# Two feed-forward blocks on one core: the down-projection of parts 2 and 3 as seven block products, added to x in DRAM

## The chip, the cores and the metric

One core of a Trainium2 chip runs the whole kernel. The metric is the device time of one execution in microseconds (us). The core has a matmul engine (PE), a vector engine (DVE), a scalar engine (ACT) and GpSimd (POOL), which all work on tiles in SBUF; PE writes its sums to PSUM banks. SP and POOL issue the transfers spoken of here.

## The reference

One layer of a language model for 512 prompt tokens and 8 sample tokens. A half-step feed-forward block stands before and after a mixer of attention and a state-space scan; only the two feed-forward blocks matter here.

```
def half_ffn(x, norm_g, w_in, w_out):
    h = rmsnorm(x, norm_g)
    gate, up = jnp.split(h @ w_in, 2, axis=-1)
    return x + FFN_RESIDUAL * ((jax.nn.silu(gate) * up) @ w_out)
...
        xp = half_ffn(xp, ffn1_norm[l], w_ffn1_in[l], w_ffn1_out[l])
...
        xp = xp + mixer_output(att, y_ssm, z, att_out_norm[l], ssm_out_norm[l], w_out[l])
...
        xp = half_ffn(xp, ffn2_norm[l], w_ffn2_in[l], w_ffn2_out[l])
```

FFN_RESIDUAL is 0.5, x has 1024 features, the hidden layer 2816, and everything is float32.

## The kernel before

x is kept transposed, as eight tiles of 128 features x 520 tokens, and the tokens are worked on in two halves of 260 (HF). A float32 product is made of three matmuls: both operands are cut into a high part (a cast by ACT) and a low part (what is left, a subtraction by DVE), and PE adds high x high, high x low and low x high in one PSUM bank. One matmul takes 128 x 128 weights and 260 columns.

A feed-forward block (`ffn_comb`) works through its 22 hidden blocks of 128 in four parts of 6, 6, 6 and 4 (PARTS). In each part the gate and up projections come first, block by block, then the down-projection of that part into all eight tiles of x. The first five hidden blocks (SFROM) are made by plain products. From the sixth on, the gate and up projections of a hidden block are one "pair": a 2 x 2 block product (two weight matrices, two token halves) of seven block products (`comb_pair`, `product`), as in the Strassen-Winograd scheme. Each of the seven has 4 x 3 = 12 matmuls; x, y and z are the PSUM banks that they add up in, tiles cx, cy and cz. ACT and DVE evict the banks between the products (L587 to L601). The fourth product of a pair is done one pair later (`comb_last`), and then ACT and DVE cut the finished hidden block into hidh and hidl (L612, L613).

The down-projection is plain: for each of eight outputs m, a loop over the hidden blocks k of the part and the two halves calls `mm3` (L222 to L224, tile fo), and DVE adds half of each bank to x (L468), which was loaded again into SBUF behind the first part (`reload`, tiles xr). That makes 8 x 6 x 2 x 3 = 288 matmuls for a part of six blocks. The last part of the first block runs with the mixer's opening (`to_mixer`, its weights in the tiles wraw, whi and wlo, L165, L191, L192); the last part of the second goes with the closing norm (`last_out`).

Weights come in units, a list made by `stream`: "cl" and "dn" plain ones, "pair" ones with seven weight combinations. A unit of a pair is loaded by SP as five raw tiles br; POOL adds up two of the sums by transfers that accumulate into SBUF (L348, L349), and DVE adds the other two (L381, L383; tile s). `b_split` cuts a unit into high parts qh (ACT, L354) and low parts ql (DVE, L355). Units are cut AHEAD = 10 us of matmul work before their use (`b_more`), and loaded at most two units ahead of the cuts. The raw tiles lie in a ring of 12, the cut ones in rings of 14 and 12 (pools pf and pg).

The order of PE's instructions is that of the program. The order on the other engines is set by a scheduler, within the dependencies, and each engine works through its row in order.

Of the kernel before, what the change touches and what calls it, by code (L numbers as in the profile page):

```python
# [14 lines left out]
T = 520  # L15
# [8 lines left out]
SRAW = 3  # L24
AHEAD = 10.0
# [57 lines left out]

def layout(inp):
# [5 lines left out]
    for n, s in (("ffn1", "1"), ("ffn2", "2")):  # L90
        out["wi" + s] = c(g[f"w_{n}_in"][0].reshape(8, 128, 2, 22, 128).transpose(3, 2, 1, 0, 4)).reshape(44, 128, 1024)
        out["wo" + s] = c(g[f"w_{n}_out"][0].reshape(22, 128, 8, 128).transpose(2, 1, 0, 3)).reshape(8, 128, 2816)
# [52 lines left out]
class Program:  # L145
# [147 lines left out]
    def stream(self, s):  # L293
# [3 lines left out]
        for lo, hi in PARTS:  # L297
            for j in range(lo, hi):
                if j < SFROM:
                    u += [("cl", wi[2 * j + i], 1024, 5.8) for i in range(2)]  # L300
                else:
                    u.append(("pair", wi[2 * j], wi[2 * j + 1], 10.1))
            if s == "1" and hi == PARTS[-1][1]:
                break
            u += [("dn", wo[m][:, lo * 128:hi * 128], (hi - lo) * 128, 0.72 * (hi - lo)) for m in range(8)]
# [6 lines left out]
    def q2(self, name):  # L312
# [6 lines left out]
        else:  # L319
            pool = self.pf if n < 12 or n % 7 % 2 == 0 else self.pg  # L320
        return pool.tile([128, 512], F32R, name=name, tag="q")

    def r2t(self, name):
        first = self.b_loaded <= 2 and self.b_first
        return (self.p0 if first else self.pf).tile([128, 512], F32, name=name, tag="r", bufs=4 if first else 12)

    def b_load(self):
# [15 lines left out]
        g, u = p  # L343
        h = slice(0, 512), slice(512, 1024)
        g0, s1, s3, g1, u1 = t = [self.r2t(f"br{n}_{i}") for i in range(5)]
# [12 lines left out]
    def b_split(self):  # L358
# [11 lines left out]
        else:  # L370
            g0, s1, s3, g1, u1 = raw
            s2, s4 = self.t2("s2"), self.t2("s4")
            w = {}
            ends = self.b_cut == len(self.bu), self.b_cut == len(self.bu) - 1
            if self.b_first == 0 and any(ends):
                self.qpool = self.pf
            w[1], w[5] = self.cut(g0), self.cut(s1)
            if self.b_first == 0 and ends[0]:
                self.qpool = self.pg
            w[2] = self.cut(g1)  # L380
            nc.vector.tensor_add(s2[:, :512], s1, g0)  # L381
            w[6] = self.cut(s2)
            nc.vector.tensor_add(s4[:, :512], s2[:, :512], g1)  # L383
            w[3], w[7] = self.cut(s4), self.cut(s3)
            if self.b_first == 0 and ends[1]:
                self.qpool = self.pg
            w[4] = self.cut(u1)
# [15 lines left out]
    def ffn_comb(self, gcol, source, after=None, early=None):  # L403
# [3 lines left out]
        with self.tc.manual_schedule(engines={mybir.EngineType.PE}):  # L407
            hid, held, r, norm = [], None, None, None
            for j in range(SFROM):
                pair = []  # L410
                if j == 0:
# [6 lines left out]
                    if self.b_first:  # L418
                        self.leave("p0")
                        self.enter("pg", 12, "right")  # L420
# [23 lines left out]
            prev = None  # L444
            for part, (lo, hi) in enumerate(PARTS):
                for j in range(max(lo, SFROM), hi):
                    prev = self.comb_pair(j, prev, hid)
                last = part == len(PARTS) - 1
# [1173 lines left out]
```

## Time and profile before

| | us |
|---|---|
| three runs | 1106.94, 1107.76 (median), 1111.99 |
| profiled execution, its own time | 1109.26 |
| its span in the profile | 1107.5 |
| PE busy | 1073.4 |
| DVE busy | 719.4 |
| ACT busy | 501.4 |
| POOL busy | 264.6 |

The first feed-forward block lies at about 5 to 374 us of the span, the mixer behind it to about 735, the second block from there to about 1092. A matmul's record lasts longer than the distance to the next one, so distances are read from starts. The time from issue to landing of a transfer counts until its end is known to the engine that waits for it.

### The profile page before, as it was taken

Reading aid. Unit: us, or ns where it says so; the run is one execution under the profiler, and the core shown is the slowest. Engines: PE = TensorE matmul, PEld = TensorE weight load, DVE = VectorE, ACT = ScalarE, POOL = GpSimd, SP = SyncE. Lnnn points to the kernel's source line nnn. Section 1 sums busy time; section 2 is a strip of 40 time slices with the busy share of each in tenths; the row PEclk is TensorE's granted clock in tenths of the full one; section 3 lists DMA queues with packets and bytes.
Section 4 is the critical chain, followed back from the end, with each engine's and each line's share of the span. In section 5 each row is a group of like instructions: output and inputs, shape, how many; then the busy total and the mean of one; then the engine's idle time right before and its main releaser. Section 6 shows DMA issues by size and latency. Waiting matters only on the chain.

```text
span 1107.5 us, 23255 instructions
## 1 busy us (share of the span) xinstructions
PE 1073.4 (97%) x9079; PEld 991.7 (90%) x9079; DVE 719.4 (65%) x1499; ACT 501.4 (45%) x1077; POOL 264.6 (24%) x261
## 2 busy tenths in 40 slices
PE   8999999999999999999999998999999999999995
PEld 6999999999999988776756676999999999999995
DVE  6985477467555679363768868449855764685563
ACT  6452355256244422456622555245534543562452
POOL 0001001110105667575343321120020011101013
PEclk9999999999999999999999999999999999999997
DMA  8539358455616788688899735163484584556302
GB/s 272 136 104 255 92 144 222 107 139 170 161 47 205 269 305 298 232 281 305 292 379 406 268 131 197 47 221 99 133 226 104 131 232 98 147 176 150 109 11 78
DMA packets 93917, 204.30 MB, mean 184 GB/s; under 512 B 13384, under 2 KB 21960, under 8 KB 89712
## 3 DMA queue, kind: packets, MB, share of 16 engines
q1 hardware_dynamic: 68736, 124.19, 34.4%
q0 software_dynamic: 22336, 77.08, 24.6%
q10 hardware_dynamic: 2736, 1.56, 0.5%
q8 instruction: 71, 1.16, 0.4%
q14 instruction: 38, 0.31, 0.1%
HBM read 191.78 MB, written 11.01 MB: 183 GB/s over the span
## 4 chain that ended last, share of the span: by engine, by line
PE 86%; DVE 5%; DMA 3%; issue 2%; ACT 2%; POOL 1%; ACTq 0%; DVEq 0%; SPq 0%; POOLq 0%
PE fo L223 7%; PE fo L224 7%; PE fo L222 7%; PE cx L578 6%; PE cx L577 6%; PE cx L576 6%; PE mps L222 4%; PE mps L223 3%; PE mps L224 3%; PE gu L222 3%; PE gu L224 3%; PE gu L223 3%; PE cy L576 3%; PE cy L577 3%; PE cy L578 3%; PE sps L1060 2%
## 5 line engine op out<-in xcount | busy, mean ns | idle before, releaser
L354 ACT CAST qh<-br 128x512 fp32r<-128x512 f32 (+1 forms) x310 | 168.2, 585 | 120.0 <-PE fo L223 57.5
L355 DVE TENSOR_TENSOR ql<-br,qh 128x512 fp32r<-128x512 f32 (+1 forms) x310 | 188.8, 644 | 44.1 <-ACT qh L354 19.3
L223 PE MATMUL fo<-hidl,qh 128*128 128x260 f32 x640 | 181.3, 283 | 0.8 <-DVE hidl L613 0.8
L222 PE MATMUL fo<-hidh,qh 128*128 128x260 f32 x640 | 181.1, 283 | 0.0
L224 PE MATMUL fo<-hidh,ql 128*128 128x260 f32 x640 | 180.8, 283 | 0.0
L578 PE MATMUL cx<-ch,ql 128*128 128x260 f32 x544 | 153.8, 283 | 0.0
L577 PE MATMUL cx<-cl,qh 128*128 128x260 f32 x544 | 153.6, 282 | 0.0
L576 PE MATMUL cx<-ch,qh 128*128 128x260 f32 x544 | 153.5, 282 | 0.0
L223 PEld LDWEIGHTS fo<-hidl,qh 128*128 128x128 f32 x640 | 120.4, 188 | 1.6 <-DVE hidl L613 1.5
L222 PEld LDWEIGHTS fo<-hidh,qh 128*128 128x128 f32 x640 | 120.5, 188 | 0.0
L224 PEld LDWEIGHTS fo<-hidh,ql 128*128 128x128 f32 x640 | 120.5, 188 | 0.0
L222 PE MATMUL mps<-hh,whi 128*128 128x260 f32 x384 | 113.3, 295 | 2.3 <-DVE raw L880 2.3
L348 POOL DMA_DIRECT2D br<-in_wi x34 | 29.7, 874 | 354.7 <-DMA br<-in_wi 204.7
L223 PE MATMUL mps<-hl,whi 128*128 128x260 f32 x384 | 109.7, 286 | 0.6 <-DVE hl L233 0.6
L224 PE MATMUL mps<-hh,wlo 128*128 128x260 f32 x384 | 109.4, 285 | 0.0
L576 PEld LDWEIGHTS cx<-ch,qh 128*128 128x128 f32 x544 | 102.4, 188 | 0.0
L578 PEld LDWEIGHTS cx<-ch,ql 128*128 128x128 f32 x544 | 102.4, 188 | 0.0
L577 PEld LDWEIGHTS cx<-cl,qh 128*128 128x128 f32 x544 | 102.3, 188 | 0.0
L786 POOL DMA_INDIRECT kv<-in_kc,ix x66 | 74.0, 1122 | 59.5 <-PE cy L578 25.7
L222 PEld LDWEIGHTS mps<-hh,whi 128*128 128x128 f32 x384 | 73.3, 191 | 13.5 <-issue 10.4
L577 PE MATMUL cy<-cl,qh 128*128 128x260 f32 x272 | 77.0, 283 | 0.0
L576 PE MATMUL cy<-ch,qh 128*128 128x260 f32 x272 | 76.9, 283 | 0.0
(430 smaller groups left out, 2705.4 us busy)
## 6 DMA issues: line engine op xcount, KB each, us to landing
br<-in_wi SPq DMA_DIRECT2D x206, 256.0 KB, 3.9
br<-in_wi POOLq DMA_DIRECT2D x68, 256.0 KB, 4.7
br<-in_wo SPq DMA_DIRECT2D x56, 256.0 KB, 2.9
wraw<-in_wm SPq DMA_DIRECT2D x24, 512.0 KB, 6.3
br<-in_wo SPq DMA_DIRECT2D x48, 128.0 KB, 2.7
kv<-in_kc SPq DMA_DIRECT2D x22, 256.0 KB, 4.6
spill<-xr SPq DMA_DIRECT2D x16, 260.0 KB, 3.3
xr<-spill SPq DMA_DIRECT2D x16, 260.0 KB, 5.5
```

The lines of the kernel that those rows point to most:

```text
L222: mm(out, lhsT=hi[:, ks], rhs=xh[:, cs], start=start, stop=False)
L223: mm(out, lhsT=hi[:, ks], rhs=xl[:, cs], start=False, stop=False)
L224: mm(out, lhsT=lo[:, ks], rhs=xh[:, cs], start=False, stop=stop)
L348: nc.gpsimd.dma_start(s1, u[:, h[1]], accum_op=ALU.add)
L354: self.nc.scalar.copy(hi[:, :n], raw[:, :n])
L355: self.nc.vector.tensor_sub(lo[:, :n], raw[:, :n], hi[:, :n])
L576: mm(out, lhsT=hi[:, ks], rhs=xh, start=start and i == 0, stop=False, skip_group_check=True)
L577: mm(out, lhsT=hi[:, ks], rhs=xl, start=False, stop=False, skip_group_check=True)
L578: mm(out, lhsT=lo[:, ks], rhs=xh, start=False, stop=i == 3, skip_group_check=True)
L786: nc.gpsimd.indirect_dma_start(out=pages[j], out_offset=None, in_=a["kc"], in_offset=bass.IndirectOffsetOnAxis(ap=self.ix[:, 4 * n + j:4 * ...
L1060: nc.tensor.matmul(self.sbank[32 * hp:32 * hp + 32, cs], lhsT=self.qz[:, c0:c0 + 32], rhs=rhs(hp), start=(n % 16 == 0), stop=(n % 16 == 15 ...
```

## The change

The down-projections of the second and third part (COMB, each six hidden blocks) of both feed-forward blocks are made of seven block products too (`down_comb`). Here the 2 x 2 blocks are two outputs m and m+1 by two hidden blocks, times two hidden blocks by two token halves. A part has three pairs of hidden blocks and four pairs of outputs; each of the seven products has 3 x 3 = 9 matmuls into the tiles dx, dy and dz. `hidden` makes the seven operand combinations from two finished hidden blocks, in place of hidh and hidl; the rows of the output weights are put into that order on the host (`hidden_order`). The work of `down_comb` stands behind the first pair of the next part, and the tail's fourth product is done within its first output pair.

The results x0 and x1 (tiles xs, a ring of four) are no longer added to x in SBUF. ACT and DVE evict them, scaled by 0.5 or -0.5, and POOL adds them to x in DRAM (`spill`) by accumulating transfers. The first part's down-projection loads each x tile for its addition and stores it to `spill`; x is reloaded from there before the last part. The products within a pair have a new order, 1, 5, (4 of the pair before), 2, 6, 3, 7, and `combos` copies one more operand (eight ACT copies). The rings shrink: raw tiles 12 to 10, cut tiles 14 to 11 and 12 to 9; xs (4) and the DVE sums (2) get rings of their own.

The core of the diff:

```
+COMB = (1, 2)
...
-            u += [("dn", wo[m][:, lo * 128:hi * 128], (hi - lo) * 128, 0.72 * (hi - lo)) for m in range(8)]
+            if part in COMB:
+                return [("pair", w[m], w[m + 1], n // 2, 1.26 * (hi - lo)) for m in range(0, 8, 2)]
+            return [("dn", w[m], n, 0.72 * (hi - lo)) for m in range(8)]
...
                 for j in range(max(lo, SFROM), hi):
-                    prev = self.comb_pair(j, prev, hid)
...
+                    prev = self.comb_pair(j, prev, hx if prev and j == lo else hid, comb)
+                    if j == lo and todo is not None:
+                        self.down_comb(hx, prev, hid)
...
+                if last:
+                    self.reload(self.spill)
...
+                    xm = self.x[m] if last else self.x_load(m, source)
...
                     if not last:
+                        nc.sync.dma_start(self.spill[m], xm[:, :T])
...
+    def down_comb(self, hx, tail, hid):
...
+        for m in range(0, 8, 2):
+            w = self.b_take()
+            x, y, z = (self.bank1(n)[:, :HF] for n in ("dx", "dy", "dz"))
+            x0, x1 = (self.px.tile([128, 528], F32, name=f"xs{m + i}", tag="x") for i in range(2))
+            pu = self.t2("pu")
+            self.product(x, w, 1, True, hx)
+            nc.scalar.copy(z, x)
+            self.product(y, w, 5, True, hx)
+            nc.scalar.activation(pu[:, a], y, AF.Copy, scale=-0.5)
+            if m == 0:
+                self.comb_last(tail, hid)
+            self.product(x, w, 6, False, hx)
+            nc.scalar.activation(pu[:, b], x, AF.Copy, scale=0.5)
+            self.product(z, w, 2, False, hx)
+            nc.scalar.activation(x0[:, a], z, AF.Copy, scale=0.5)
+            self.product(x, w, 7, False, hx)
+            stt(x1[:, b], x, -0.5, pu[:, a], ALU.mult, ALU.add)
+            self.product(y, w, 3, False, hx)
+            stt(x0[:, b], y, 0.5, pu[:, b], ALU.mult, ALU.add)
+            nc.gpsimd.dma_start(self.spill[m], x0[:, :T], accum_op=ALU.add)
+            self.product(x, w, 4, False, hx)
+            nc.scalar.activation(x1[:, a], x, AF.Copy, scale=-0.5)
+            nc.gpsimd.dma_start(self.spill[m + 1], x1[:, :T], accum_op=ALU.add)
+            self.b_more()
...
+    def hidden(self, c, hx):
...
+        x0, x1 = hx.pop()[0], c
+        p1 = self.t2("p1", F32R)
+        nc.scalar.copy(p1[:, a], x0[:, a])
+        nc.vector.tensor_sub(p1[:, b], x0[:, a], p1[:, a])
+        s, t = self.t2("hs"), self.t2("ht")
+        nc.vector.tensor_sub(s[:, a], x0[:, a], x0[:, b])
+        nc.vector.tensor_sub(s[:, b], x1[:, b], x0[:, b])
+        nc.vector.scalar_tensor_tensor(t[:, a], s[:, b], -1.0, x0[:, a], ALU.mult, ALU.subtract)
+        nc.vector.scalar_tensor_tensor(t[:, b], t[:, a], -1.0, x1[:, a], ALU.mult, ALU.subtract)
+        q = self.two(s, x1, t)
```

How it moves the rows, at three places. First ACT in the first block, down-projection of part 2. Before, the row there is casts of weights alone (br raw tiles, s sums of them):

```order
196 L354 CAST qh<-br_1_2701 128x512 [waits DMASW6_49,Activation_49]
197 L354 CAST qh<-br_3_2703 128x512 [waits DMAHW0_49,PE_49,Activation_49]
198 L354 CAST qh<-s_2812 128x512 [waits DVE_49,PE_49,Activation_49]
199 L354 CAST qh<-s_2813 128x512 [waits DVE_49,PE_49,Activation_49]
200 L354 CAST qh<-br_2_2702 128x512 [waits DMASW7_49,PE_49,Activation_49]
201 L354 CAST qh<-br_4_2704 128x512 [waits DMAHW2_49,PE_49]
202 L354 CAST qh<-br_1_2761 128x512 [waits DMASW0_49,PE_49,Activation_49]
```

Now, from the end of the pair ahead on, with the first evictions of the first output pair:

```order
211 L374 CAST qh<-br_1_2540 128x384 [waits DMASW2_49,PE_49]
212 L374 CAST qh<-br_3_2542 128x384 [waits DMAHW2_49,PE_49,Activation_49]
213 L374 CAST qh<-s_2714 128x384 [waits PE_49]
214 L526 COPY dz<-dx 128x260
215 L374 CAST qh<-s_2715 128x384 [waits DVE_49,PE_49]
216 L528 ACTIVATE pu<-dy 128x260
217 L374 CAST qh<-br_2_2541 128x384 [waits DMASW3_49,PE_49]
218 L532 ACTIVATE pu<-dx 128x260 [waits PE_49]
219 L534 ACTIVATE xs_2761<-dz 128x260 [waits PE_49]
```

The evictions of dx, dy and dz stand between the casts of the weights for the next units, and a cast that waits for PE is ahead of the copy into dz.

Second POOL at the same place. Before, it issues only the accumulating transfers for weight sums:

```order
22 L348 DMA br_1_2701<-in_wi 128x512 [waits DMAHW3_49,DMAHW7_49,DMASW3_49,DVE_49]
23 L349 DMA br_2_2702<-in_wi 128x512 [waits DMAHW1_49,DMAHW5_49,DMASW7_49,DVE_49]
24 L348 DMA br_1_2761<-in_wi 128x512 [waits DMAHW0_49,DMAHW4_49,DMASW5_49,DVE_49]
25 L349 DMA br_2_2762<-in_wi 128x512 [waits DMAHW2_49,DMAHW6_49,DMASW1_49,DVE_49]
26 L348 DMA br_1_2845<-in_wi 128x512 [waits DMAHW1_49,DMAHW5_49,DMASW2_49,DVE_49]
```

Now those and the additions to x in DRAM take turns:

```order
30 L368 DMA br_1_2747<-in_wo 128x384 [waits DMAHW3_49,DMASW2_49,DVE_49]
31 L539 DMA spill<-xs_2761 128x520 [waits DVE_49,Activation_49]
32 L369 DMA br_2_2748<-in_wo 128x384 [waits DMAHW5_49,DMASW3_49]
33 L542 DMA spill<-xs_2762 128x520 [waits Activation_49]
34 L368 DMA br_1_2882<-in_wi 128x512 [waits DMAHW0_49,DMASW4_49,DVE_49]
35 L539 DMA spill<-xs_2896 128x520 [waits DVE_49,Activation_49]
36 L369 DMA br_2_2883<-in_wi 128x512 [waits DMAHW2_49,DMASW5_49]
37 L542 DMA spill<-xs_2897 128x520 [waits Activation_49]
```

Each addition to x waits for evictions by ACT or DVE, and the next transfer for a weight sum stands behind it.

Third SP's queue at the end of the first block, where the weights of the last down-projection (wraw) are loaded. Before, they follow the raw tiles of the last pair:

```order
232 L347 DMA br_3_4348<-in_wi 128x512 [waits DMAHW5_49,DVE_49,Activation_49]
233 L347 DMA br_2_4347<-in_wi 128x512 [waits DMAHW6_49,DMASW4_49,Activation_49]
234 L347 DMA br_4_4349<-in_wi 128x512 [waits DMAHW7_49,DVE_49,Activation_49]
235 L165 DMA wraw_4734<-in_wo 128x512 [waits DMAHW0_49,DMASW6_49,DMAHW3_49,DVE_49,Activation_49]
236 L165 DMA wraw_4736<-in_wo 128x512 [waits DMAHW1_49]
```

Now the eight reloads of x stand ahead of them:

```order
249 L367 DMA br_2_4534<-in_wi 128x512 [waits DMAHW6_49,DMASW0_49,DVE_49]
250 L367 DMA br_4_4536<-in_wi 128x512 [waits DMAHW7_49,DVE_49]
251 L1551 DMA xr_4975<-spill 128x520 [waits DMAHW0_49,DMASW3_49,PE_49]
252 L1551 DMA xr_4976<-spill 128x520 [waits DMAHW1_49,DMASW5_49,PE_49]
253 L1551 DMA xr_4977<-spill 128x520 [waits DMAHW2_49,DMASW7_49,PE_49]
254 L1551 DMA xr_4978<-spill 128x520 [waits DMAHW3_49,DMASW1_49,PE_49]
255 L1551 DMA xr_4979<-spill 128x520 [waits DMAHW4_49,DMASW3_49,PE_49]
256 L1551 DMA xr_4980<-spill 128x520 [waits DMAHW5_49,DMASW5_49,PE_49]
257 L1551 DMA xr_4981<-spill 128x520 [waits DMAHW6_49,DMASW7_49,PE_49]
258 L1551 DMA xr_4982<-spill 128x520 [waits DMAHW7_49,DMASW1_49,PE_49]
259 L175 DMA wraw_4999<-in_wo 128x512 [waits DMAHW0_49,DMASW4_49,DVE_49]
```

The first load of wraw waits for DVE in both; its place in the memory of the cut tiles is another one now, because the rings are shorter, and the DVE instruction that frees it is the low part of the last pair's last cut.

## Rows read from the trace of the kernel before

**Rows 1.** Page: busy us of each engine, then the chain that ended last.

```profile
PE 1073.4 (97%) x9079; PEld 991.7 (90%) x9079; DVE 719.4 (65%) x1499; ACT 501.4 (45%) x1077; POOL 264.6 (24%) x261
...
PE 86%; DVE 5%; DMA 3%; issue 2%; ACT 2%; POOL 1%; ACTq 0%; DVEq 0%; SPq 0%; POOLq 0%
```

**Rows 2.** Page, costliest groups: busy us, mean ns, idle before; L222 and L224 alike.

```profile
L223 PE MATMUL fo<-hidl,qh 128*128 128x260 f32 x640 | 181.3, 283 | 0.8 <-DVE hidl L613 0.8
L222 PE MATMUL fo<-hidh,qh 128*128 128x260 f32 x640 | 181.1, 283 | 0.0
```

**Rows 3.** Timeline of PE, first matmuls of products: start us, duration us.

```profile
147.49 0.28 PE L576 MATMUL cy<-ch,qh 128*128 128x260 f32 x1
...
148.94 0.28 PE L576 MATMUL cz<-ch,qh 128*128 128x260 f32 x1
...
151.81 0.28 PE L576 MATMUL cx<-ch,qh 128*128 128x260 f32 x1
```

**Rows 4.** Windows, one pair and one down-projection: us, busy, clock, DMA share, GB/s.

```profile
134.50:144.60 10.10, 10.10 (x86) 10.10 (x85) 7.67 (x15) 6.13 (x13) 0.86 (x1) 1.00 0.58 158
...
182.09:215.90 33.81, 33.81 (x281) 33.81 (x282) 16.26 (x33) 7.60 (x14) 5.02 (x6) 1.00 0.59 131
```

**Rows 5.** Timeline of PE, start of part 2's down-projection, idle in brackets.

```profile
181.32 0.28 PE L222 MATMUL fo<-hidh,qh 128*128 128x260 f32 x1
182.09 0.39 PE L223 MATMUL fo<-hidl,qh 128*128 128x260 f32 x1 [0.49 <-DVE hidl L613]
```

**Rows 6.** Timeline of ACT in the same pair as rows 3.

```profile
147.47 0.61 ACT L354 CAST qh<-br 128x512 fp32r<-128x512 f32 x1
147.99 0.37 ACT L587 COPY cz<-cx 128x260 f32<-128x260 f32 x1
...
152.01 0.38 ACT L593 COPY pu<-cx 128x260 f32<-128x260 f32 x1 [0.98 <-PE cx L578]
```

**Rows 7.** Groups of 100 to 340 us by form: busy us, mean ns.

```profile
L354 ACT CAST qh<-br 128x512 fp32r<-128x512 f32 x93 | 54.2, 619 | 36.3 <-PE fo L223 17.9 <-issue 13.5 <-PE fo L224 3.0
L354 ACT CAST qh<-br 128x256 fp32r<-128x256 f32 x16 | 6.5, 403 | 4.7 <-DMA br<-in_wi 2.4 <-PE fo L223 2.2
...
L355 DVE TENSOR_TENSOR ql<-br,qh 128x512 fp32r<-128x512 f32 x95 | 62.0, 684 | 13.8 <-PE fo L224 4.9 <-ACT qh L354 3.8 <-issue 1.8
L468 DVE SCALAR_TENSOR_TENSOR xr<-fo,xr 128x260 f32<-128x260 f32 x44 | 17.0, 424 | 17.0 <-PE fo L224 17.0
L355 DVE TENSOR_TENSOR ql<-br,qh 128x256 fp32r<-128x256 f32 x16 | 6.7, 417 | 1.7 <-PE cx L577 1.4 <-issue 0.3
```

**Rows 8.** Line L165 at 330 to 360 us: the last part's weight loads.

```profile
L165 SPq DMA_DIRECT2D wraw<-in_wo x7: 327/338/423, 337.5 to 357.4; - x7
...
DMA to landing us min/median/max: 4.3/4.4/4.4
```

**Rows 9.** Timeline of PE, first matmul of the first block's last down-projection.

```profile
347.42 0.28 PE L222 MATMUL fo<-hidh,whi 128*128 128x260 f32 x1
```

**Rows 10.** Page, DMA queues and issues (KB each, us to landing).

```profile
q1 hardware_dynamic: 68736, 124.19, 34.4%
q0 software_dynamic: 22336, 77.08, 24.6%
...
br<-in_wi SPq DMA_DIRECT2D x206, 256.0 KB, 3.9
br<-in_wi POOLq DMA_DIRECT2D x68, 256.0 KB, 4.7
br<-in_wo SPq DMA_DIRECT2D x56, 256.0 KB, 2.9
...
spill<-xr SPq DMA_DIRECT2D x16, 260.0 KB, 3.3
xr<-spill SPq DMA_DIRECT2D x16, 260.0 KB, 5.5
```

**Rows 11.** Page, costliest groups: POOL issuing the weight sums, 874 ns each.

```profile
L348 POOL DMA_DIRECT2D br<-in_wi x34 | 29.7, 874 | 354.7 <-DMA br<-in_wi 204.7
```

More of the change, by code (lines that the diff above doesn't have):

```diff
@@ L81, in shape_constants, with hidden_order @@
     return f, b.astype(mybir.dt.np(BF16)), i3, r
+def hidden_order():
+    o = []
+    for part, (lo, hi) in enumerate(PARTS):
+        o += [j for i in range(2) for j in range(lo + i, hi, 2)] if part in COMB else range(lo, hi)
+    return o
 def layout(inp):
@@ L296, in stream, with down @@
         u = []
-        for lo, hi in PARTS:
+        def down(part):
+            lo, hi = PARTS[part]
+            n = 128 * (hi - lo)
+            w = [wo[m][:, lo * 128:hi * 128] for m in range(8)]
+            if part in COMB:
+                return [("pair", w[m], w[m + 1], n // 2, 1.26 * (hi - lo)) for m in range(0, 8, 2)]
+            return [("dn", w[m], n, 0.72 * (hi - lo)) for m in range(8)]
+        for part, (lo, hi) in enumerate(PARTS):
             for j in range(lo, hi):
@@ L301, in stream @@
                 else:
-                    u.append(("pair", wi[2 * j], wi[2 * j + 1], 10.1))
-            if s == "1" and hi == PARTS[-1][1]:
-                break
-            u += [("dn", wo[m][:, lo * 128:hi * 128], (hi - lo) * 128, 0.72 * (hi - lo)) for m in range(8)]
+                    u.append(("pair", wi[2 * j], wi[2 * j + 1], 512, 10.1))
+                if j == lo and part - 1 in COMB:
+                    u += down(part - 1)
+            if part not in COMB and not (s == "1" and hi == PARTS[-1][1]):
+                u += down(part)
         self.bu = u
@@ L324, in r2t @@
         first = self.b_loaded <= 2 and self.b_first
[L325 removed]
+        return (self.p0 if first else self.pf).tile([128, 512], F32, name=name, tag="r", bufs=4 if first else 10)
     def b_load(self):
@@ L567, in combos, with product @@
         halves(self.two(*tt), 6, 4)
-    def product(self, out, w, p, start):
+    def product(self, out, w, p, start, blocks):
         mm = self.nc.tensor.matmul
         hi, lo = w[p]
-        for i in range(4):
-            xh, xl = self.cx[i][p]
+        last = len(blocks) - 1
+        for i, block in enumerate(blocks):
+            xh, xl = block[p]
             ks = slice(128 * i, 128 * i + 128)
@@ L577, in product, with comb_pair @@
             mm(out, lhsT=hi[:, ks], rhs=xl, start=False, stop=False, skip_group_check=True)
-            mm(out, lhsT=lo[:, ks], rhs=xh, start=False, stop=i == 3, skip_group_check=True)
-    def comb_pair(self, j, prev, hid):
+            mm(out, lhsT=lo[:, ks], rhs=xh, start=False, stop=i == last, skip_group_check=True)
+    def comb_pair(self, j, prev, hid, comb):
         nc = self.nc
@@ L1575, in early @@
             def early():
+                self.leave("py")
                 self.leave("pg")
@@ L1601, in run @@
                 self.ffn_comb(V_F2, self.spill)
-            self.leave("pg")
-            self.leave("pf")
+            for n in ("py", "pg", "px", "pf"):
+                self.leave(n)
 def kernel(**inputs):
```

111 lines of the change are left out of this document (72 added, 39 removed).

## The prediction, made before the changed kernel had run

> **What bounds the kernel now.** I read the page's engine shares and its chain first [rows 1]: the matmul engine is busy 97% of the span and 86% of the chain that ended last lies on it. So in the two feed-forward stages time is the number of matmuls times their pitch, unless something makes PE wait. Then the costliest groups [rows 2]: the down-projection is three groups of 640 matmuls, with 0.8 us of waiting in all. The 283 ns printed there overlap, so they are not the price of one. The price is in the timeline of a block product [rows 3]: 12 matmuls from 147.49 to 148.94, and 12 more to each next start (151.81 is two products later), so 1.44 us / 12 = **0.120 us** each. Last I looked at what DVE and ACT do in a stretch of pairs and in a down-projection [rows 4], because the change buys matmuls with work on those two.
>
> **What it removes.** A down-projection of six hidden blocks is 8 outputs x 6 blocks x 2 halves x 3 = 288 matmuls; in seven products it is 4 output pairs x 7 products x 3 block pairs x 3 = 252. Parts 2 and 3 of both stages do it: 4 x 36 = 144 matmuls fewer, 144 x 0.120 = **-17.3 us**. All 144 stood in stretches where PE hardly waited, so all of it is on the path. At the old down-projection of part 2 PE also waited at 181.32 to 182.09 for the last hidden block's low part [rows 5], 0.77 instead of 0.12: **-0.65 us**, since the products now run one pair later, when the hidden blocks have long been ready.
>
> **What it adds to the path: evictions in less cover.** Within a pair, a product that starts from an evicted bank has one product of 12 matmuls as cover, 1.44 us. ACT's copy starts 0.20 us after the next product's first matmul (152.01 against 151.81) and lasts 0.38 [rows 3, 6]; when a cast is ahead of it, it starts later (147.99 against 147.49, behind the cast of 147.47) and ends at 148.36, 0.87 us after the product's end, 0.58 before it is needed at 148.94. In the new down-projection a product has 9 matmuls, 1.08 us. The order of ACT shows the tight spot: a cast of a weight sum, then the copy of dx into dz, which the sixth product, on the same bank, needs. By the analogue the margin is 1.08 - 0.87 = 0.21 us, less if the cast (384 columns, between 0.403 and 0.619 us [rows 7], estimate 0.51) is itself released late: it waits for a DVE sum or for a slot that the first product frees. It is tight in 12 of the 16 output pairs (in the other four the tail's product stands between). Bounds: 0 where the margin holds; a whole cast late, 0.51 x 16 = 8 us. The analogue row, which holds, is nearer: I take **+1.5 us**. The other evictions have a product or more of cover and no cast that must be ahead.
>
> **The step into the mixer.** Before, the first weight of the last down-projection was issued at 337.5 and landed 4.4 us later, though its first matmul came only at 347.42: 5 us of slack [rows 8, 9]. After, the order of SP's queue has that load behind the eight reloads of x and on a wait for DVE, and the wait resolves to the low part of the last unit's last cut, whose slot (of 9 instead of 12) is freed by the product into cz of the last pair. From that product's end to the first down matmul there are 3 products and a matmul, 37 x 0.120 = 4.5 us. What has to fit: the cut 0.69, issue about 0.1, landing 4.4, the cast 0.62 and the subtraction 0.69 [rows 7, 8], 6.5 us, and the low part is wanted two matmuls after the high one, at 4.7. So it is about 6.5 - 4.7 = **+1.8 us** late, once (the second stage takes its last weights another way); 0 if the landing is the 2.9 of other such loads [rows 10] and the cut is early, 3 at most if DVE is late by another instruction or two.
>
> **What lies under other work, at nothing.** (1) DVE. Two hidden blocks were two subtractions of 520 columns, about 0.69 each; now five of 260 (0.424 each, by the eviction's row) and three of 520: 4.2 against 1.4 us, +1.4 per pair. A pair had 7.67 of 10.10 us busy, so 9.1 of 10.1: 90%. In a down-projection an output pair costs seven subtractions and two sums of 384 columns (0.55 each, estimate between 0.417 and 0.684) and two evictions, 5.8 of its 63 x 0.120 = 7.56 us [rows 4, 7]. These records overlap at their ends, so both fit; what covers them is the look-ahead of about one pair (10 us) in the cut weights, and when it is gone each pair loses what DVE is over. (2) ACT: seven casts of 0.51 and five copies of 0.38 are 5.5 of 7.56 us. The eight copies added where the first stage's products are set up cost 8 x 0.38 = 3 us of ACT, beside a longer DVE chain. (3) Transfers. An output pair loads five tiles of 0.197 MB, accumulates into two of them, and sends two tiles of 0.266 MB to x. At what the queues did while busy (124.19 MB in 34.4% of 1107.5 us, 0.326 MB/us; 77.08 MB in 24.6%, 0.283 MB/us [rows 10]) that is 0.98/0.326 + 0.93/0.283 = 6.3 of 7.56 us: 83%, against 59% in the old down-projection [rows 4]. No row shows an accumulate whose destination is DRAM. From below, it costs no more than a plain store, 3.3 us to landing; from above, twice the time on the engines for reading and writing there: 1.9 us more per output pair, 8.2 of 7.56, a deficit of 2.5 us over the four, under the look-ahead. I take nothing, as stores to DRAM landed sooner (3.3) than loads from it (5.5) [rows 10]. The Trainium skill speaks against that ("DMA: Bandwidth & Descriptors", section "Anatomy of one DMA — SWDGE (gpsimd) path"): a transfer reports done only when its last byte is confirmed, and this "can cause a surprisingly long delay especially when the write target is HBM"; the trace's 3.3 against 5.5 us doesn't show it for stores. (4) POOL: 0.874 us per issue [rows 11], four per output pair, 3.5 of 7.56 us; a spill accumulate waits for its evictions and holds the next weight accumulate behind it for some 2 to 3 us, which the look-ahead also covers. (5) The shorter ring of raw tiles (10 for 12, two units): a load can start only a unit ahead, about 10 us, and needs 3.9 to 4.7 [rows 10] and the accumulates behind it as much again: 1 to 2 us to spare.
>
> **Sum.** -17.3 - 0.65 + 1.5 + 1.8 = -14.65 us. The profiled execution took 1109.26 us (span 1107.5 and 1.76 around it), so 1094.6; the median of the three runs is 1107.76, 1.5 less, which gives **1093 us**.
>
> **Rivals.**
> A, the forecast, with its bounds: losses of 0 to 11 us instead of 3.3. At nothing it is 1089.8; the runs of before spread from 1106.94 to 1111.99, so 1087 to 1099. Chance 0.62.
> B, PE stutters at the evictions: cover of 1.08 us is too little not at one product in seven but at two, 0.4 us each, 16 output pairs: +13 over the clean 1089.8, about 1103 (1099 to 1106). For it: 0.21 us is all the margin, and a cast ahead holds the copy, as at 147.99. Against: ACT is busy only 73% there. Chance 0.16.
> C, DVE or the transfers become the bound and the saved matmuls turn into waits: DVE at 90% in a pair, where it must also answer PE; if each of the 24 pairs in the four parts loses 0.7 us, 17 us are given back and nothing is won, about 1106 to 1109. This is also the case in which the change does what it says, and it doesn't matter. Against: DVE sat idle 2.4 us of each pair before. Chance 0.13.
> D, slower: the accumulates into DRAM land late. The ring for their sources has four tiles, two per output pair, so a tile is wanted again 2 x 7.56 = 15.1 us after its first write; some 3 us go to the other eviction and the issue, so up to 12 us to landing costs nothing. The nearest rows are 3.3 (store) and 4.7 (accumulate into SBUF) [rows 10], and both would have to be far off. From 12 us it decides: ACT's and DVE's evictions wait for the tile, their casts queue behind, PE runs dry. At 20 us the last two output pairs of each part wait 8 us, times 4 is 32, less if the look-ahead eats some: 1089.8 + 32 = about 1120. By the page of the Trainium skill named above, a destination in HBM would push towards this. Chance 0.09.
>
> **How the numbers follow.** The forecast is A's 1093. The range must leave out no more than two in ten: from 1087 to 1106 it takes A and B and leaves C's half and D above. Half a per cent, what a measurement of this kernel can tell from no change, is 1102.2 to 1113.3: A and a part of B fall below it, the rest of B and C inside, D above. Faster 0.76, same 0.15, slower 0.09.
>
> **What would show it.** Right: 144 matmuls fewer, pitch 0.120 in the groups of the new down-projection, an output pair of 7.6 us, a wait of 1 to 2 us before the first matmul of the last part in the first stage, small gaps at the sixth product released by ACT's copy into dz. Wrong: gaps at other products (B), PE waiting for the low parts of weights with DVE busy without a break (C), ACT or DVE idle on the spill accumulate and its landing far above 5 us (D). What would break the forecast most is a transfer to DRAM that adds at another speed than it stores.

## The result

The changed kernel is slower. Its runs have a median of 1115.51 us (1111.28 to 1124.27, 17 runs), the kernel before one of 1107.82 us in 17 runs; the ratio is 1.0069 with a 95% interval of 1.0049 to 1.0088, so 8 us lost where 15 were forecast to be won. The time lies outside the range that I gave. The profiled execution has a span of 1117.9 us; its own time, 1119.96 us, is 4.5 us above the median, so its waits are somewhat longer than those of a middle run.

The page of the changed kernel: busy us of each engine, the DMA queues (packets, MB, share of 16 engines), the chain that ended last, the transfers (KB each, us to landing). They answer to [rows 1] and [rows 10].

```profile
PE 1066.6 (95%) x8935; PEld 980.2 (88%) x8935; DVE 778.8 (70%) x1619; ACT 570.4 (51%) x1245; POOL 319.2 (29%) x325
...
q1 hardware_dynamic: 75648, 135.85, 37.3%
q0 software_dynamic: 31552, 91.90, 32.9%
...
PE 76%; DMA 9%; DVE 6%; issue 4%; POOL 3%; ACT 2%; DVEq 0%; SPq 0%; ACTq 0%; POOLq 0%
...
br<-in_wi SPq DMA_DIRECT2D x206, 256.0 KB, 4.4
br<-in_wi POOLq DMA_DIRECT2D x68, 256.0 KB, 5.3
...
spill<-xs POOLq DMA_DIRECT2D x32, 260.0 KB, 7.4
```

The 144 matmuls are gone (8935 against 9079), yet PE's share of the chain fell from 86% to 76%, and DMA's rose from 3% to 9%. So PE now waits. The list of waits says for whom (us in total, times, longest); first PE's two that were not there before, then DVE's behind them:

```profile
PE dx L654 <- DVE xs L536: 11.9, 6, 3.7
PE cx L654 <- DVE pu L678: 5.3, 4, 2.0
```

```profile
DVE s L402 <- DMA br<-in_wi: 40.6, 13, 5.9
```

The first line of PE's is in the new down-projections; the second is in the gate/up pairs, and comes back below. The largest wait of all, at the last output pair of the first block's part 2, shows the whole chain. PE, then DVE, then POOL, from the timeline (start us, duration us, idle before in brackets; rows left out between):

```profile
217.61 0.28 PE L656 MATMUL dy<-ch,ql 128*128 128x260 f32 x1
221.63 0.39 PE L654 MATMUL dx<-ch,qh 128*128 128x260 f32 x1 [3.73 <-DVE xs L536]
```

```profile
213.27 0.69 DVE L375 TENSOR_TENSOR ql<-s,qh 128x512 fp32r<-128x512 f32 x1 [0.40 <-ACT dz L526]
218.01 0.69 DVE L402 TENSOR_TENSOR s<-br,br 128x512 f32<-128x512 f32 x1 [4.05 <-DMA br<-in_wi]
...
221.15 0.42 DVE L536 SCALAR_TENSOR_TENSOR xs<-dx,pu 128x260 f32<-128x260 f32 x1
```

```profile
207.19 0.86 POOL L369 DMA_DIRECT2D br<-in_wi  x1 [3.32 <-DMA br<-in_wi]
207.72 1.23 POOL L542 DMA_DIRECT2D spill<-xs  x1
210.52 0.86 POOL L368 DMA_DIRECT2D br<-in_wi  x1 [1.57 <-DVE ql L375]
211.17 1.12 POOL L539 DMA_DIRECT2D spill<-xs  x1
```

Read from the end: product 4 can't add to bank dx before DVE has evicted what product 7 left there (L536). That eviction is 0.42 us long, but in DVE's row it stands behind a weight sum for a gate/up pair (L402), and that sum waits for its raw tile: the accumulating transfer issued at 210.52 had landed only by 218.01, 7.5 us later. PE stands still for 3.73 us. Not all of DVE's 4.05 us is the transfer's: POOL had itself waited 1.57 us for a cut by DVE before it issued it, and with a landing of 4.7 us, the median of [rows 10], DVE would by estimate still have waited some 1.3 us. Then a second price, in the windows (us, busy of PE, PEld, DVE, ACT, POOL, granted clock, DMA share, GB/s):

```profile
217.60:221.60 4.00, 0.29 (x3) 0.08 (x1) 3.55 (x7) 0.62 (x1) 0.86 (x1) 1.00 1.12 235
221.60:223.00 1.40, 1.37 (x11) 1.38 (x12) 1.40 (x3) 0.11 (x1) 0.00 (x0) 0.95 1.09 189
223.00:226.30 3.30, 3.30 (x17) 3.30 (x17) 0.80 (x2) 2.02 (x5) 2.06 (x3) 0.50 0.91 297
```

After the wait the granted clock is 0.50, the 1.2 GHz level, for 3.3 us: 15 or 16 matmuls at 0.216 in place of 0.120 us, 1.5 us more. And the DMA share is 1.12 and 1.09 up to then and 0.91 behind it (records overlap, so it can pass 1): the engines are full.

The waits for pu (L678, 5.3 us) are DVE's eviction of the seventh product of a gate/up pair, which the pair's fourth product needs. The new order of products leaves two products of 12 matmuls for it, 2.9 us, or two of 9, 2.2 us, where a down-projection begins; the old order left four of 12, 5.8 us. One of the four, 1.53 us at 856.69, comes before the first new down-projection of its block (914.35), where nothing is added to x in DRAM yet. So a part of the loss is shorter cover in the pairs themselves. No run put the old order of products back.

### The profile page after: what moved, and what is told of

Same layout as the page of the kernel before. It is cut to its first block, busy times and chain, and to the rows that moved or that the text cites. A ratio compares the mean times of both kernels' runs of the same rounds, so it can differ in the third digit from the quotient of the medians.

```text
span 1117.9 us, 23706 instructions
## 1 busy us (share of the span) xinstructions
PE 1066.6 (95%) x8935; PEld 980.2 (88%) x8935; DVE 778.8 (70%) x1619; ACT 570.4 (51%) x1245; POOL 319.2 (29%) x325
## 4 chain that ended last, share of the span: by engine, by line
PE 76%; DMA 9%; DVE 6%; issue 4%; POOL 3%; ACT 2%; DVEq 0%; SPq 0%; ACTq 0%; POOLq 0%
PE cx L654 6%; PE cx L655 6%; PE cx L656 6%; PE gu L232 4%; PE gu L233 4%; PE gu L234 3%; DMA br<-in_wi 3%; PE fo L233 3%; PE cy L654 3%; PE cy L656 3%; PE cy L655 3%; PE fo L234 3%; PE fo L232 3%; PE mps L232 2%; PE mps L233 2%
## 5 line engine op out<-in xcount | busy, mean ns | idle before, releaser
L375 DVE TENSOR_TENSOR ql<-br,qh 128x512 fp32r<-128x512 f32 (+2 forms) x326 | 205.2, 642 | 75.8 <-ACT qh L374 30.5
L374 ACT CAST qh<-br 128x512 fp32r<-128x512 f32 (+2 forms) x326 | 186.3, 583 | 139.5 <-PE fo L234 29.3
L655 PE MATMUL cx<-cl,qh 128*128 128x260 f32 x408 | 115.3, 283 | 0.0
L656 PE MATMUL cx<-ch,ql 128*128 128x260 f32 x408 | 115.2, 282 | 0.0
L375 DVE TENSOR_TENSOR ql<-s,qh 128x512 fp32r<-128x512 f32 (+1 forms) x100 | 63.7, 644 | 22.8 <-ACT qh L374 8.5
L656 PE MATMUL cy<-ch,ql 128*128 128x260 f32 x272 | 77.0, 283 | 0.0
L655 PE MATMUL cy<-cl,qh 128*128 128x260 f32 x272 | 76.9, 283 | 0.0
L655 PEld LDWEIGHTS cx<-cl,qh 128*128 128x128 f32 x408 | 76.8, 188 | 0.0
L233 PEld LDWEIGHTS mps<-hl,whi 128*128 128x128 f32 x384 | 73.1, 190 | 1.2 <-DVE hl L243 1.1
L233 PE MATMUL fo<-hidl,qh 128*128 128x260 f32 x256 | 72.6, 284 | 0.7 <-DVE hidl L694 0.7
L234 PEld LDWEIGHTS mps<-hh,wlo 128*128 128x128 f32 x384 | 72.9, 190 | 0.0
L232 PE MATMUL fo<-hidh,qh 128*128 128x260 f32 x256 | 72.7, 284 | 0.0
```

What stands on the lines that cost most here:

```text
L232: mm(out, lhsT=hi[:, ks], rhs=xh[:, cs], start=start, stop=False)
L233: mm(out, lhsT=hi[:, ks], rhs=xl[:, cs], start=False, stop=False)
L234: mm(out, lhsT=lo[:, ks], rhs=xh[:, cs], start=False, stop=stop)
L374: self.nc.scalar.copy(hi[:, :n], raw[:, :n])
L375: self.nc.vector.tensor_sub(lo[:, :n], raw[:, :n], hi[:, :n])
L655: mm(out, lhsT=hi[:, ks], rhs=xl, start=False, stop=False, skip_group_check=True)
```

## The experiments

Three theories stood at the start. T: the transfers fill the engines. Q: POOL's row holds weight sums back behind the additions to x. R: the shorter rings. B, the burst, is T made sharper after the first four runs.

**Additions to x cut to 16 columns.**

```
-            nc.gpsimd.dma_start(self.spill[m], x0[:, :T], accum_op=ALU.add)
+            nc.gpsimd.dma_start(self.spill[m][:, :16], x0[:, :16], accum_op=ALU.add)
...
-            nc.gpsimd.dma_start(self.spill[m + 1], x1[:, :T], accum_op=ALU.add)
+            nc.gpsimd.dma_start(self.spill[m + 1][:, :16], x1[:, :16], accum_op=ALU.add)
```

> The changed kernel with each of the 32 additions to x in DRAM cut to 16 of its 520 columns; the rest of the sum is left out. Order, issues and waits on POOL stay. Theory T (transfers): an accumulating packet of 2080 bytes holds its DMA engine 180 to 200 ns against 85 for a plain one, so the additions fill the engines just when the next pairs' weights come; without their bytes (50 us of engine time) the weight tiles are on time, DVE's wait for br at its weight sums falls from 41 us to under 20, PE's waits for the evictions xs and pu (17 us) go, time about 1095 to 1100. Theory Q (POOL's order): the waits of the additions hold back the weight accumulates queued behind them; these waits stay, so the time stays within 5 us of 1115. Theory R (rings): the shorter rings are the cause; time stays near 1115.

Measured: 1099.76 us, ratio to before 0.9933 (0.9908 to 0.9957). The row of POOL with its waits is the same, only bytes went, and 16 us with them. T holds here, Q and R don't. It held less cleanly than forecast: DVE still waits 20.5 us for raw tiles, just over the 20 named, and PE still 6.1 us for evictions (3.4 for xs, 2.7 for pu), all of PE's in the second block.

**Additions as plain stores.**

```
-            nc.gpsimd.dma_start(self.spill[m], x0[:, :T], accum_op=ALU.add)
+            nc.gpsimd.dma_start(self.spill[m], x0[:, :T])
...
-            nc.gpsimd.dma_start(self.spill[m + 1], x1[:, :T], accum_op=ALU.add)
+            nc.gpsimd.dma_start(self.spill[m + 1], x1[:, :T])
```

> The changed kernel with the 32 additions to x in DRAM as plain stores of the same bytes from the same queue; the sum is left out. T: engine time of these bytes halves (50 to about 23 us), so a part of the loss goes: 1098 to 1108. Q and R: within 5 us of 1115. If the price were the landing in DRAM and not the accumulating, the time would stay near 1115 too.

Measured: 1111.35 us, 1.0024 (1.0000 to 1.0047): about 4 us back of 16, less than T said, and within the 5 us around 1115 that Q, R and a price of the landing in DRAM allowed. By itself this run speaks for none of them. Half the engine time of these bytes may not be enough to take the engines off their limit, which is why I looked at what else is loaded there.

**The kernel before with the short rings.**

```
-            pool = self.pf if n < 12 or n % 7 % 2 == 0 else self.pg
+            pool = self.pf if n < 8 or n % 7 % 2 == 0 else self.pg
...
-        return (self.p0 if first else self.pf).tile([128, 512], F32, name=name, tag="r", bufs=4 if first else 12)
+        return (self.p0 if first else self.pf).tile([128, 512], F32, name=name, tag="r", bufs=4 if first else 10)
...
-            self.enter("pf", 14)
+            self.enter("pf", 11)
...
-            self.enter("pg", 12, "right")
+            self.enter("pg", 9, "right")
```

> The kernel before with the rings of the changed one (raw tiles 10 for 12, cut tiles 11 and 9 for 14 and 12) and nothing else. R: it loses most of what the change lost, 1118 or more. T and Q: at most 3 us over 1107.8, since no transfer is added.

Measured: 1109.45 us, 1.0004 (0.9988 to 1.0021). The rings cost nothing by themselves, so R falls as a cause of its own. The changed kernel with the old, longer rings was not tried.

**The down-projections' weight sums by POOL's adder.**

```
-        nc.gpsimd.dma_start(s1, u[:, h[1]], accum_op=ALU.add)
-        nc.gpsimd.dma_start(s3, g[:, h[0]], accum_op=ALU.add)
+        if w < 512:
+            nc.gpsimd.tensor_add(s1, s1, u1)
+            nc.gpsimd.tensor_add(s3, s3, g0)
+        else:
+            nc.gpsimd.dma_start(s1, u[:, h[1]], accum_op=ALU.add)
+            nc.gpsimd.dma_start(s3, g[:, h[0]], accum_op=ALU.add)
```

> The changed kernel with the two accumulated weight sums of each output pair of the down-projections made by POOL's adder instead of accumulating transfers; the additions to x stay. T: 43 us of engine time go and a sum is ready about 1 us after its tile instead of 5: 1100 to 1108. Q: POOL still waits at the additions to x with the sums behind: near 1115. R: near 1115. If POOL's adder slows DVE, DVE's means rise and the time stays.

Measured: 1120.04 us, 1.0107 (1.0074 to 1.0140), 4.5 us more than the changed kernel in the median, with intervals that overlap. The 6.3 MB that no longer accumulate won nothing. The DMA share fell at the first output pair of the down-projection, where there was room, and not at the last two. The windows of the first and of the last, in the changed kernel and then in this one (the DMA share is the last number but one):

```profile
186.28:193.88 7.60, 7.60 (x66) 7.60 (x65) 6.39 (x16) 4.76 (x12) 1.72 (x2) 1.00 0.76 176
...
216.68:224.28 7.60, 3.87 (x28) 3.66 (x27) 5.06 (x9) 2.67 (x6) 1.76 (x3) 0.91 1.10 248
```

```profile
186.71:194.31 7.60, 7.60 (x66) 7.60 (x65) 6.19 (x14) 4.99 (x12) 3.42 (x2) 1.00 0.46 132
...
217.11:224.71 7.60, 4.08 (x25) 3.87 (x24) 5.06 (x9) 2.01 (x4) 2.35 (x3) 0.77 1.07 234
```

This run changed two things at once. POOL's adder slowed DVE: in 186 to 320 us the mean of DVE's subtraction of 384 columns rose from 552 to 630 ns, and DVE's busy time from 99.5 to 104.9 us. DVE's wait for raw tiles fell from 40.6 to 24.7 us, yet PE still waited 14.5 us for xs. So the time alone decides nothing about T. What the windows suggest is that the engine time that hurts is that of other bytes: those of the next gate/up pairs, which are loaded two units ahead of their cut, in the middle of the down-projection. That is theory B, and the next runs test it.

**The pairs' weight sums left out.**

```
-        nc.gpsimd.dma_start(s1, u[:, h[1]], accum_op=ALU.add)
-        nc.gpsimd.dma_start(s3, g[:, h[0]], accum_op=ALU.add)
+        if w < 512:
+            nc.gpsimd.dma_start(s1, u[:, h[1]], accum_op=ALU.add)
+            nc.gpsimd.dma_start(s3, g[:, h[0]], accum_op=ALU.add)
```

> The changed kernel with the accumulated weight sums of the gate/up pairs left out (the raw tile is used as it is); those of the down-projection and all additions to x stay. Theory B (burst): what fills the engines in the down-projection is the weights of the next pairs, five plain tiles at 3.4 us of 16 engines and two accumulating ones at 2.9, one such unit per 7.6 us output pair, together with 2.9 us of additions to x: 9.1 us for 7.6. Without the sums it is 6.3 of 7.6, the tiles are on time: DVE's wait for br under 15 us, PE's waits for xs and pu nearly gone, 1095 to 1100. Theory S (additions alone are at fault, by their own landing or their place on POOL): stays above 1108.

Measured: 1099.57 us, 0.9933 (0.9910 to 0.9957). DVE's wait for raw tiles is nearly gone:

```profile
DVE s L403 <- DMA br<-in_wi: 5.7, 3, 2.9
```

Taking away either half of what accumulates, the additions to x or the pairs' sums, gives the same 16 us. It needs both to pass the limit, as B says; S, the additions alone, falls. One reservation: without the sums a raw tile also no longer has POOL's issue and a second landing behind its load, so DVE's wait had to shrink whether the engines are full or not. Cutting the additions and splitting the down-projection (below) don't have that flaw.

**Both left out.**

> The changed kernel with the additions to x cut to 16 of 520 columns and the pairs' weight sums left out, both at once: the parts of the result that rest on them are left out. If the transfers are all that stands between the forecast and the result, this is the forecast's clean case with the late first weight: 1107.8 - 17.3 - 0.65 + 1.8 = 1091.7, so 1090 to 1095, and no PE waits for xs or pu. If evictions in short cover or DVE's load also cost something by themselves, it stays at 1097 to 1100 like the kernels with one of the two.

The edits of the first experiment and of the one just above, together. Measured: 1099.28 us, 0.9923 (0.9894 to 0.9951): not the 1091.7 of the clean case, and no better than with one of the two. So the transfers account for 16 us, and some 8 more have another cause. PE's timeline shows most of it. First matmul behind the tail (the sixth product's, of the first output pair), and first matmul behind the down-projection, in both blocks (these are part 2's; L655 is the product's line in this kernel):

```profile
190.67 0.28 PE L655 MATMUL dx<-ch,qh 128*128 128x260 f32 x1
...
219.42 0.29 PE L655 MATMUL cx<-p,qh 128*128 128x260 f32 x1
...
904.09 0.28 PE L655 MATMUL dx<-ch,qh 128*128 128x260 f32 x1
...
933.84 0.28 PE L655 MATMUL cx<-p,qh 128*128 128x260 f32 x1
```

Between them lie 252 - 18 = 234 matmuls, 28.1 us at 0.120; it took 28.75 and 29.75. With the two of part 3 (28.9 and 29.55) that is 4.6 us, lost at short gaps of 0.1 to 0.4 us at evictions. The late first weight costs 1.5 here. And the second block's first down-projection, whose matmuls the change leaves alone, loses about 2 us at its last hidden block, where the kernel before loses 0.1 and the changed kernel 0.8; why it does here is not settled. From 1107.8 - 17.3 - 0.65 = 1089.85, these three make about 1098.

**Product 4 later.** It goes behind the second product of the next output pair.

```
+            else:
+                late()
             self.product(x, w, 6, False, hx)
...
-            self.product(x, w, 4, False, hx)
-            nc.scalar.activation(x1[:, a], x, AF.Copy, scale=-0.5)
-            nc.gpsimd.dma_start(self.spill[m + 1], x1[:, :T], accum_op=ALU.add)
+            def late(m=m, w=w, x=x, x1=x1):
+                self.product(x, w, 4, False, hx)
+                nc.scalar.activation(x1[:, a], x, AF.Copy, scale=-0.5)
+                nc.gpsimd.dma_start(self.spill[m + 1], x1[:, :T], accum_op=ALU.add)
```

> The changed kernel with the fourth product of an output pair moved behind the second product of the next one (of the last output pair: of the next gate/up pair), so that DVE's eviction of the seventh has 3.2 us of cover, not 1.1. No transfer changes. If an eviction that stands in DVE's row behind a weight sum waiting for its transfer is how lateness reaches PE: each of the some six waits for xs loses up to 2.2 us and the clock's falls behind them go, 1105 to 1110, with DVE's wait for br unchanged near 41 us. If lateness reaches PE by missing weights anyway: 1113 to 1117.

Measured: 1106.62 us, 0.9993 (0.9969 to 1.0016): 9 us back with the same transfers, as expected if lateness reaches PE through the eviction. DVE's wait for raw tiles didn't stay at 41 us, it fell to 27.6; I had not expected that, and 27.6 is close to what the kernel before has. That row I had not shown, and it matters:

```profile
DVE s L381 <- DMA br<-in_wi: 28.2, 6, 7.4
```

Before, DVE waited 28 us for raw tiles too, up to 7.4 us at once, and PE lost nothing by it: no PE wait for DVE longer than 0.5 us stands in its down-projections ([rows 5] is the largest). An output had its own two banks there, and at least the 4.3 us of the next output's matmuls went by before anybody missed them. So two thirds of the lateness (28 of 41 us) are old; what is new is that an eviction with 1.1 us of cover, or 2.2 to 2.9 in the pairs, stands behind it.

**The down-projection split in two.**

```
-                if j == lo and part - 1 in COMB:
-                    u += down(part - 1)
+                if j - lo < 2 and part - 1 in COMB:
+                    u += down(part - 1)[2 * (j - lo):2 * (j - lo) + 2]
...
-                    if j == lo and todo is not None:
-                        self.down_comb(hx, prev, hid)
-                        hx, todo, prev = [], None, None
+                    if j - lo < 2 and todo is not None:
+                        self.down_comb(hx, prev, hid, 4 * (j - lo))
+                        prev = None
+                        if j > lo:
+                            hx, todo = [], None
```

The second pair's hidden block is finished behind the last output pair, since its operands need the slots of the old ones.

> The changed kernel with the down-projection split: two output pairs behind the first gate/up pair of the next part, two behind the second. Same work, same transfers, spread: two output pairs and a pair need 2 x 4.8 + 6.2 + 4 x 1.44 = 21.6 us of engine time in 25.2 us. B: the burst is flattened, 1098 to 1106. S: near 1113.

Measured: 1100.57 us, 0.9948 (0.9926 to 0.9971), with every addition and sum in place. Its waits of DVE:

```profile
DVE s L402 <- DMA br<-in_wi: 13.5, 6, 4.4
```

PE's waits for xs and pu fell from 17.2 to 2.8 us. The bytes are the same; only their order in time is another. B holds again.

**All sums by POOL's adder.**

```
-        nc.gpsimd.dma_start(s1, u[:, h[1]], accum_op=ALU.add)
-        nc.gpsimd.dma_start(s3, g[:, h[0]], accum_op=ALU.add)
+        nc.gpsimd.tensor_add(s1, s1, u1)
+        nc.gpsimd.tensor_add(s3, s3, g0)
```

> The changed kernel with all accumulated weight sums, of pairs and of down-projections, made by POOL's adder from tiles that are loaded anyway; additions to x stay. B: engine time of the burst falls as in the kernel without sums, and a sum is ready 1.4 us behind its tile: 1095 to 1103. If POOL's adder is slow beside DVE (1.3 to 2.0 us seen for 384 columns) or POOL's row is held up by waits, the sums are as late as before: 1110 to 1120. S: 1110 to 1115.

The five loads of a unit also come in another order, u1 before g1 and s3 (not shown). Measured: 1119.37 us, 1.0122 (1.0085 to 1.0159). Relieving the engines this way fails, and DVE's groups in 186 to 320 us say why (busy us, mean ns of one, idle before). The changed kernel, then this one:

```profile
L375 DVE TENSOR_TENSOR ql<-br,qh 128x512 fp32r<-128x512 f32 x36 | 24.3, 685 | 10.0 <-ACT qh L374 5.5 <-PE cx L655 2.3 <-PE dx L655 1.9
...
L402 DVE TENSOR_TENSOR s<-br,br 128x512 f32<-128x512 f32 x8 | 5.5, 687 | 9.5 <-DMA br<-in_wi 9.5
```

```profile
L375 DVE TENSOR_TENSOR ql<-br,qh 128x512 fp32r<-128x512 f32 x36 | 31.8, 898 | 3.4 <-PE dx L655 2.8 <-ACT qh L374 0.5
...
L402 DVE TENSOR_TENSOR s<-br,br 128x512 f32<-128x512 f32 x8 | 7.6, 944 | 0.5
```

The sums no longer wait for transfers, but the same subtraction takes 898 ns in place of 685 beside POOL's adder, and DVE has hardly any idle time left: it is busy for 123.6 of these 134 us, against 99.5.

**Split and product 4 later, together.** The two edits above in one kernel; the fourth product of each half's last output pair goes into the gate/up pair that follows:

```
-                        self.down_comb(hx, prev, hid, 4 * (j - lo))
-                        prev = None
+                        prev = self.down_comb(hx, prev, hid, 4 * (j - lo))
```

> The split down-projection together with the later fourth product. B with the lateness reaching PE through evictions: the rest of the waits for xs and pu (some 4 us with the clock) shrinks, 1096 to 1100. If what is left is the first weight of the last part and the mixer's own scatter: same as the split one, 1100.

Measured: 1099.1 us, 0.9906 (0.9879 to 0.9932): faster than the kernel before by 0.9%, and the lowest median with the whole computation. From the split alone (0.9926 to 0.9971) it is not told apart, and both outcomes named beforehand fit it. **The same with weights cut 13 us ahead:**

```
-AHEAD = 10.0
+AHEAD = 13.0
```

> The same with weights cut 13 us of work ahead of their use, not 10. If the tiles still come late at times and the rings have room, 1 to 3 us less than with 10. If the rings are full anyway, or casts get in the way of evictions, the same or up to 5 us more.

Measured: 1102.86 us, 0.9955 (0.9935 to 0.9976). More look-ahead doesn't help; which of the two reasons named it is was not tried.

## Why the prediction was wrong

The matmuls: right. 144 fewer, at the same 0.120 us; the wait of [rows 5] is gone from the start of part 2.

The transfers, priced at nothing: **the step that failed.** Three things in it were wrong.

First the price of a byte. I divided a queue's bytes by its busy share over the whole span, 0.283 MB/us for q0. But that queue also carries plain gathers. In the old down-projection alone, where it only accumulates, the trace of before had this (window 182.09 to 215.9: packets, MB, share):

```profile
q0 software_dynamic: 1006, 1.83, 33.0%
q1 hardware_dynamic: 1394, 2.55, 25.9%
```

1.83 MB in 33.0% of 33.8 us is 0.164 MB/us; the plain ones, 2.55 MB in 25.9%, are 0.29. An accumulating byte holds the engines about twice as long. In the changed kernel, 201.5 to 222.8 us, it is 0.176:

```profile
q0 software_dynamic: 1488, 2.70, 71.9%
q1 hardware_dynamic: 1455, 2.64, 35.6%
```

Second which bytes. I counted the down-projection's own weights for each output pair. What is loaded during the last output pairs is the next pairs' weights, since loading runs two units ahead of the cuts: five tiles of 0.262 MB at 0.35 MB/us (2.64 MB in 35.6% of 21.3 us), two accumulating ones and two additions to x, 1.06 MB at 0.176. That is 3.8 + 6.0 = 9.8 us for an output pair of 7.56: 130%, where I had 83%.

Third the cover. I said that the look-ahead of 10 us in cut weights hides late tiles. It does, for the weights: by the list of waits PE never waits for a low or high part of them in the new down-projections. It doesn't for an eviction that stands in DVE's row behind the sum of a unit which is needed only much later.

The transfers together: 1115.5 with them, 1099.3 without the additions and sums, 16 us. By the same figures an output pair asks for 8.6 us of its 7.56 when the additions are plain stores (estimate: 3.8 for five tiles, 3.0 for two sums at 0.176, 1.8 for 0.53 MB at 0.29), and for 6.8 without them, which fits the 4 and the 16 us that came back. What stays open: the additions and the sums share the queue q0, and no run tells the order within that queue from the engines being full (71.9% and 35.6% together, above).

In the profiled execution the parts about add up (estimate): 1109.26 - 17.95 for the clean case, 17.2 of waits for xs and pu, some 3 for the clock behind two of them, 4.6 of short gaps as measured with both left out, 1.7 at the step into the mixer, 1118 of 1119.96.

Evictions in less cover: the mechanism that I described was there, and of the size that I gave. With both kinds of accumulation left out, the sixth product starts late behind ACT's copy into dz, which stands behind casts of weight sums (the matmul ahead of this one started at 213.38):

```profile
212.22 1.13 ACT L375 CAST qh<-s 128x512 fp32r<-128x512 f32 x2
213.25 0.38 ACT L527 COPY dz<-dx 128x260 f32<-128x260 f32 x1
```

```profile
213.68 0.39 PE L655 MATMUL dx<-ch,qh 128*128 128x260 f32 x1
...
916.81 0.39 PE L655 MATMUL dx<-ch,qh 128*128 128x260 f32 x1 [0.21 <-DVE xs L537]
```

Counted from the starts of the first two matmuls of each product, 1.5 of the 4.6 us stand there, for a term of 1.5. Another 2.3 stand at the fourth product, behind DVE's eviction of the seventh, as at 916.81, and 0.7 at the seventh, behind one by ACT. So what failed here is the sentence that the other evictions have "a product or more of cover and no cast that must be ahead": I had asked only what stands ahead of the evictions in ACT's row. What decided was what stands ahead of them in DVE's, cuts and sums that wait for transfers: 17.2 us of PE's waits in the changed kernel, for which the sum has no term. Two slips beside it changed nothing: the upper bound takes 16 output pairs where 12 were named as tight (6 us, not 8), and most of B's chance is counted as faster, though its middle, 1103, lies above 1102.2.

The step into the mixer: right, +1.8 forecast. The last cut ends at 346.6, the load is issued at 346.7 and lands 4.5 us later, and PE waits as [rows 8] and [rows 9] let expect:

```profile
345.93 0.69 DVE L375 TENSOR_TENSOR ql<-br,qh 128x512 fp32r<-128x512 f32 x1 [0.40 <-issue]
...
351.44 0.39 PE L232 MATMUL fo<-hidh,whi 128*128 128x260 f32 x1 [1.15 <-ACT whi L201]
...
352.17 0.39 PE L234 MATMUL fo<-hidh,wlo 128*128 128x260 f32 x1 [0.22 <-DVE wlo L202]
```

Their starts are 1.43 and 0.50 us behind the matmul ahead of each, 0.12 of which is the pitch: 1.7 us.

DVE and ACT as such: right that they fit; in the windows of output pairs above DVE is busy 5.1 to 6.4 of 7.6 us, and in a pair (240.00 to 250.10) 9.67 of 10.10, for 9.1 forecast. POOL's row (4): no cost of its own shown, since cutting the bytes alone brought the gain. The rings (5): nothing by themselves, with the change not tried.

The rivals: D had the right sign and the wrong mechanism. The additions land 7.4 us behind their issue (median), below the 12 from which the ring of xs would block; neither ACT nor DVE waited for that ring. The Trainium skill ("DMA: Bandwidth & Descriptors", section "Anatomy of one DMA — SWDGE (gpsimd) path") warns of a surprisingly long delay when the write target is HBM. As plain stores from the same queue they took 6.1, and accumulating into SBUF 5.3 us, so the runs show no delay of the size that D needs. C was nearest: it named transfers as a bound, and its 17 us of waits are about PE's 17.2 for xs and pu. That the sizes agree is luck, since it looked for them at late weights in all 24 pairs; they stand behind evictions, and C had nothing for the clock's fall, the short gaps and the late first weight on top. B looked at ACT. Its place, the evictions, was where the time went.

## What to carry to other kernels

Price an accumulating transfer by a stretch in which its queue does nothing else, and count what is loaded during a stretch, not what the stretch consumes. A product chain that reuses a bank makes an eviction urgent; look at everything ahead of it in its engine's row, above all at instructions that wait for transfers, and give it more cover or spread the loads. Late tiles that cost nothing today are found in the waits of an engine off the critical path, and they are the first thing to check when the slack behind them is taken away.

## What the runs showed of the hardware

An accumulating transfer moves 0.16 to 0.18 MB in a us in which all 16 engines work on it, a plain one 0.29 to 0.35, and it makes little difference to that whether it adds into SBUF (0.164, where nothing else accumulated) or also into DRAM (0.176). By single packets of 2048 bytes, each on one engine, in the changed kernel's trace (199 to 225 us) the medians are 178 ns accumulating and 84 plain.

POOL's adder slows DVE beside it: the subtraction of 512 columns from 685 to 898 ns, the sum from 687 to 944. The Trainium skill ("SBUF — State Buffer", section "Who interferes with whom") says that a DVE instruction with two SBUF inputs contends with a GpSimd instruction that reads SBUF; these two have two such inputs, so the trace agrees. Over that whole trace the 65 of these subtractions (from raw tiles) that overlap a POOL addition in time took 1156 ns on the mean, the other 165 took 688. Not every such instruction was slowed: the other sum, L404, kept 690 ns in 186 to 320 us. The evictions from PSUM (L536) kept their 420 ns.

A wait of PE of 3.73 us was followed by 3.3 us at a granted clock of 0.50: from start to start PE lost 3.9 us by the wait (4.02 less the pitch) and 1.5 more at the lower clock. The wait of 3.32 us that ended at 318.66 had such a fall too; the next longest, 2.63 us to 940.55, had none:

```profile
318.40:321.80 3.40, 3.14 (x14) 3.14 (x15) 1.83 (x4) 2.14 (x5) 0.28 (x1) 0.51 0.88 200
940.55:944.00 3.45, 3.45 (x28) 3.34 (x28) 2.51 (x5) 1.28 (x3) 0.00 (x0) 1.00 1.06 262
```
